# Inverse square roots of the query and key scales by Newton steps on VectorE, no row form of the first norm, and four PSUM banks for the first two projections

## The chip, the cores and the metric

The kernel runs on one core of a Trainium2 chip. A core has five engines that work side by side, each through a queue of its own in order: TensorE (PE in the profile, with its weight loads apart as PEld), VectorE (DVE), ScalarE (ACT), GpSimd (POOL) and SyncE (SP, which only issues DMA transfers here). Matmul results lie in PSUM, which has eight banks; everything else lies in SBUF.

The metric is the device time of one execution in microseconds (us). The kernel before takes 1255.68 us, the median of three runs (1253.61 to 1256.59).

## The reference

A causal two-layer trunk over 512 tokens of width 1024, in float32. Layer 0 mixes tokens by attention, layer 1 by a gated short convolution; each is followed by a gated MLP of width 2816 with a width-3 causal convolution. What the change touches is the entrance of layer 0:

```python
def rms_norm(x, g):
    y = x * lax.rsqrt(jnp.mean(x * x, axis=-1, keepdims=True) + EPS)
    return y * g

xn = rms_norm(h, norm_g)                      # over 1024 features
proj = xn @ w_in                              # 1024 x (3*1024 + 8)
q, k, v = heads(...)                          # 16 heads of 64
q_fox = rms_norm(q[:, :8], fox_q_g)           # over 64 features, per head and token
k_fox = rms_norm(k[:, :8], fox_k_g)           # the same for the 8 stick-breaking heads
```

Heads 0 to 7 do softmax attention with a forget-gate decay added to the logits; heads 8 to 15 do stick-breaking attention, whose weights are a running product of sigmoids from the diagonal backwards. Every one of the later norms (before each MLP and before the convolution mixer) is the same `rms_norm`.

## The kernel before, in words

**Precision.** Each float32 matrix product is made of three fast matmuls: both factors are split into a high part (a rounded copy, by ACT) and a low part (the rest, by DVE), and high x high, high x low and low x high are added up in PSUM (`mm3`, `mm3_rhs`; L248, L473). A weight slice of 512 KB comes by DMA into a tile `raw` and is split into `whi` (L228) and `wlo` (L235). Each of these three has three buffers.

**Entrance.** x is loaded token by token and turned feature by feature by PE transposes (`take`, L672), each into a PSUM bank: tag `b` (four banks) for features 0 to 3, 6 and 7, tag `c` (two banks) for 4 and 5. Tag `a` has two banks. `keep` (L681) copies the bank to the residual stream `h` and so frees it. The norm's gain is multiplied into the split activations `hs_hi` and `hs_lo`; its scale per token, `norm.col`, is applied later, to the products. ACT sums the squares (`squares`, L688); `Norm.scale` (L280) makes the mean on DVE and calls `rsqrt`, which is one GpSimd instruction, a power of -0.5 (L313). For every norm, `spread` (L287) then turns the column of scales into a row by four PE transposes into a `c` bank (L291) and an ACT copy (`nrow`, L292). The rows of the later norms scale the projections of their layers (L774, L814 to L821). The scales of the first norm are used as a column only (L465, L481, L510), and by `rx2`, their squares over 64 (L480).

**Groups of heads.** Sixteen heads are four groups of four. Group g has three projections: `heads(0, g)` and `heads(1, g)` (keys and queries: 0 is keys) and `values(g)`, each over four blocks of 128 tokens and eight slices of features (`columns`, L446). Each block takes a PSUM bank of tag `a`. In `heads`, ACT copies the finished block out (L504) and squares it (L505), and DVE adds the squares per head (L507). At the end come two small DVE steps (L517, L518), the power on GpSimd (16 numbers on each partition, L519), and then, in `scale`, the product with `norm.col` (L510) and the scaling of both halves (L513). `turn_heads(p)` transposes a pair of heads (L530) and splits it (L534, L535). `logits`, `turn` and `weigh` are the attention steps of half a pair: logits in the `b` banks, softmax or the running product (L569 to L586), transposes of the weights in the `c` banks (L604), their split (L606, L609), and the product with the values (L628).

**What sets the order.** The source counts a clock of its own: every block of matmuls adds its estimated time (`spend`), `after(us, fn)` puts a step off until so much of that clock has gone by, and `flush` runs at once all that was put off. `scale` is put off by SCALE = 8.0. The attention steps u = 0 to 17 follow one another, and between them `fill(us)` draws as much work from a list of fillers: `values(0)`, then keys, queries and values of groups 1 to 3, then half of the output projection. `need(what)` draws fillers, half a microsecond at a time, until a step that it waits for has been written out. So:

```python
after(SCALE, scale)                   # L520, at the end of heads
need(("normed", i, p // 2))           # L526, at the head of turn_heads
```

The order of writing is not the order of an engine's queue. The framework plans each engine's queue with a cost model of its own: of the instructions that its model holds to be ready it takes the one written first, so that an instruction that isn't ready lets later ones pass. Once planned, the queue is fixed, and the chip waits wherever the model was too hopeful.

After the attention (`output(1)`, L764) come the MLP of layer 0, the convolution mixer and the MLP of layer 1.

Of the kernel before, what the change touches and what calls it, by code (L numbers as in the profile page):

```python
# [17 lines left out]
F32 = mybir.dt.float32  # L18
F32R = mybir.dt.float32r
BF16 = mybir.dt.bfloat16  # L20
I32 = mybir.dt.int32
# [4 lines left out]
P = 128  # L26
S = 512
NB = S // P
# [8 lines left out]
AHEAD = 2  # L37
PT = 2
PRE = 6.0
SCALE, SHARES, LATER = 8.0, 1.5, 1.5  # L40
SUM_STEP = 0.6
WARM = 34
HEADS = 4.0
# [5 lines left out]
def trunk(  # L49
# [71 lines left out]
    for i in range(2):  # L121
# [1 line left out]
        pool.memset(m, 0.0)  # L123
        pool.affine_select(out=m, in_=m, pattern=[[-1, P]], compare_op=ALU.is_ge, fill=MASKED, base=-i, channel_multiplier=1)
        masks.append(m)
    minus_half = const.tile([P, 16], F32, tag="minus_half", name="minus_half")
    pool.memset(minus_half, -0.5)
    ones = const.tile([P, 1], F32, tag="ones", name="ones")
    pool.memset(ones, 1.0)

# [50 lines left out]
    def after(us, fn):  # L181
        later.append((clock[0] + us, len(later), fn))
        later.sort(key=lambda e: e[0])
# [76 lines left out]
    class Norm:  # L260
# [19 lines left out]
        def scale(self, sums):  # L280
            v = tiny.tile([P, NB], F32, tag="nv", name=f"nv_{self.name}")
            dve.tensor_scalar(v, sums, 1.0 / D, EPS, op0=ALU.mult, op1=ALU.add)
            self.col = const.tile([P, NB], F32, tag="ncol", name=f"ncol_{self.name}", bufs=2)
            rsqrt(self.col, v)
            after(NROWS, self.spread)

        def spread(self):  # L287
            self.row = work.tile([P, S], F32, tag="nrow", name=f"nrow_{self.name}", bufs=1)
# [20 lines left out]
                    after(SUM_STEP, lambda: sums(b + 1, t))  # L309
            after(NSUMS, lambda: sums(0, bank("c")))  # L310

    def rsqrt(dst, v):
        pool.tensor_tensor(dst, v, minus_half[:, 0:v.shape[1]], op=ALU.pow)  # L313

    def split(hi, lo, src):
        act.activation(hi, src, AF.Copy)  # L316
# [126 lines left out]

    v_tiles = {}

    def columns(g, width=256):  # L446

        ws = [weights(), weights(AHEAD - 1)]
        for b in range(NB):
            acc = bank("a")  # L450
            tok = slice(b * P, (b + 1) * P)
            for k in range(ND):
                w = ws[k // 4]
                mm3_rhs(acc[:, 0:width], (hs_hi[:, k, tok], hs_lo[:, k, tok]), (w[0][:, k % 4, :], w[1][:, k % 4, :]), k == 0, k == ND - 1)
                spend(0.36)
                yield b, acc, k == ND - 1
# [37 lines left out]
    def heads(i, g):  # L494

        kept = [work.tile([P, 2, 256], F32, tag=("u0", "u1")[i], name=f"qk{i}{g}{j}", bufs=2 + i) for j in range(2)]
        total, r = (tiny.tile([P, NB, 4], F32, tag=n, name=f"{n}{i}{g}") for n in ("qv", "qr"))
        for b, acc, last in columns(g):
            yield 1
            if not last:  # L500
                continue
            if b % 2 == 0:
                sq = work.tile([P, S], F32, tag="sq", name=f"sq_{i}{g}{b}").rearrange("p (b h d) -> p b h d", b=2, d=HD)
            act.activation(kept[b // 2][:, b % 2, :], acc[:, 0:256], AF.Copy)  # L504
            act.activation(sq[:, b % 2], acc[:, 0:256].rearrange("p (h d) -> p h d", d=HD), AF.Square)  # L505
            if b % 2:
                dve.tensor_reduce(total[:, b - 1:b + 1, :], sq, axis=AX.X, op=ALU.add)  # L507

        def scale():
            dve.tensor_tensor(r, r, norm.col[:, :, None].to_broadcast([P, NB, 4]), op=ALU.mult)  # L510
            for j, t in enumerate(kept):
                t = t.rearrange("p b (h d) -> p b h d", d=HD)
                dve.tensor_tensor(t, t, r[:, 2 * j:2 * j + 2, :, None].to_broadcast([P, 2, 4, HD]), op=ALU.mult)  # L513
            normed[i, g] = kept
            done.add(("normed", i, g))

        dve.tensor_tensor(total, total, rx2[:, :, None].to_broadcast([P, NB, 4]), op=ALU.mult)  # L517
        dve.tensor_scalar(total, total, EPS, None, op0=ALU.add)  # L518
        rsqrt(r.rearrange("p b h -> p (b h)"), total.rearrange("p b h -> p (b h)"))  # L519
        after(SCALE, scale)  # L520

    def turn_heads(p):
# [377 lines left out]
```

## Time and profile before

| | |
|---|---|
| median of three runs | 1255.68 us |
| the profiled execution | 1255.41 us, of which the span from first to last instruction is 1253.7 us |
| PE busy | 1212.9 us (97% of the span) |
| DVE busy | 747.1 us (60%) |
| ACT busy | 500.5 us (40%) |
| POOL busy | 49.6 us (4%) |
| mean granted TensorE clock | 0.986 |
| the power (L313) with 16 numbers a partition, x8 | median 2900 ns, 24.8 us together |
| the power with 4 numbers a partition, x4 | median 1007 ns, 4.1 us together |

A row of the timeline gives the start in us from the first instruction, the duration, the engine, the line, the operation with its tiles, and how often it was repeated; in square brackets stands how long the engine had been idle, and whose end released it. A row of the windows gives for a stretch of the span its length, then for PE, PEld, DVE, ACT and POOL the busy time with the number of instructions, then the TensorE clock that was granted (1.00 is full speed), the share of the DMA engines and GB/s.

### The profile page before, as it was taken

What the parts mean: (1) busy time and instruction counts of PE and PEld (TensorE: products, weight loads), DVE (VectorE), ACT (ScalarE), POOL (GpSimd) and SP (SyncE); (2) the same over time, 40 slices, a digit from 0 to 9 for tenths busy, and PEclk for the clock granted to TensorE, in tenths of its full rate; (3) what the DMA queues carried; (4) which work ended last, traced back from release to release, by engine and by line L of the source; (5) the groups of instructions that cost most, each with busy time, mean ns of one, the idle gap of its engine ahead of it and who ended that gap; (6) DMA issues with size and microseconds to landing.
All of it is one profiled execution on the core that took longest, in us unless ns stands there. A gap on an engine that the chain in (4) does not pass through costs nothing.

```text
span 1253.7 us, 15395 instructions
## 1 busy us (share of the span) xinstructions
PE 1212.9 (97%) x6133; PEld 1008.8 (80%) x6133; DVE 747.1 (60%) x1104; ACT 500.5 (40%) x815; POOL 49.6 (4%) x114
## 2 busy tenths in 40 slices
PE   7989999987999999999999999999999999999998
PEld 7978988766888888888888888888888888888886
DVE  4575677886676777765333455555667777772312
ACT  5454566554444344443222222233343444432120
POOL 3211111100000000000000000000000000000000
PEclk8998999997999999999999999999999999999999
DMA  5321221210323333333333323323233333332330
GB/s 157 93 61 34 69 62 40 68 51 18 100 85 101 95 91 101 88 93 93 93 93 97 101 85 100 99 87 100 85 101 96 89 101 89 96 101 84 104 115 34
DMA packets 175272, 108.15 MB, mean 86 GB/s; under 512 B 4604, under 2 KB 168492, under 8 KB 175200
## 3 DMA queue, kind: packets, MB, share of 16 engines
q1 hardware_dynamic: 174944, 107.01, 28.7%
q8 instruction: 48, 0.79, 0.3%
q0 software_dynamic: 256, 0.16, 0.1%
q14 instruction: 24, 0.20, 0.0%
HBM read 105.06 MB, written 2.10 MB: 85 GB/s over the span
## 4 chain that ended last, share of the span: by engine, by line
PE 87%; DVE 7%; ACT 3%; POOL 1%; DMA 1%; issue 1%; SPq 0%; DVEq 0%; ACTq 0%
PE psb L250 11%; PE psb L252 11%; PE psa L250 11%; PE psb L251 11%; PE psa L252 11%; PE psa L251 11%; PE psa L474 4%; PE psa L476 4%; PE psa L475 4%; PE psb L474 2%; PE psb L475 2%; PE psb L476 2%; DVE rest L585 2%; POOL qr L313 1%; PE psc L604 1%; PE psb L552 1%
## 5 line engine op out<-in xcount | busy, mean ns | idle before, releaser
L228 ACT ACTIVATE whi<-raw 128x1024 fp32r<-128x1024 f32 (+2 forms) x198 | 208.4, 1053 | 357.8 <-PE psb L251 131.1
L235 DVE TENSOR_TENSOR wlo<-raw,whi 128x1024 fp32r<-128x1024 f32 (+2 forms) x198 | 240.3, 1214 | 178.1 <-ACT whi L228 177.3
L250 PE MATMUL psb<-hs_hi,whi 128*128 128x512 f32 x480 | 189.9, 396 | 0.0
L252 PE MATMUL psb<-hs_hi,wlo 128*128 128x512 f32 x480 | 189.8, 395 | 0.0
L251 PE MATMUL psb<-hs_lo,whi 128*128 128x512 f32 x480 | 188.7, 393 | 0.0
L250 PE MATMUL psa<-hs_hi,whi 128*128 128x512 f32 x416 | 164.7, 396 | 0.0
L252 PE MATMUL psa<-hs_hi,wlo 128*128 128x512 f32 x416 | 164.2, 395 | 0.0
L251 PE MATMUL psa<-hs_lo,whi 128*128 128x512 f32 x416 | 163.9, 394 | 0.0
L324 DVE SCALAR_TENSOR_TENSOR u<-y,taps,u 128x510 f32<-128x510 f32 (+1 forms) x176 | 131.0, 747 | 3.0
L474 PE MATMUL psa<-whi,hs_hi 128*128 128x256 f32 (+1 forms) x384 | 114.0, 298 | 3.8 <-ACT sq L505 1.9
L476 PE MATMUL psa<-whi,hs_lo 128*128 128x256 f32 (+1 forms) x384 | 110.9, 289 | 0.0
L475 PE MATMUL psa<-wlo,hs_hi 128*128 128x256 f32 (+1 forms) x384 | 110.6, 288 | 0.0
L251 PEld LDWEIGHTS psb<-hs_lo,whi 128*128 128x128 f32 x480 | 90.1, 188 | 21.4
L252 PEld LDWEIGHTS psb<-hs_hi,wlo 128*128 128x128 f32 x480 | 90.1, 188 | 21.4
L250 PEld LDWEIGHTS psb<-hs_hi,whi 128*128 128x128 f32 x480 | 90.3, 188 | 20.3
L252 PEld LDWEIGHTS psa<-hs_hi,wlo 128*128 128x128 f32 x416 | 78.1, 188 | 18.6
L251 PEld LDWEIGHTS psa<-hs_lo,whi 128*128 128x128 f32 x416 | 78.1, 188 | 18.4
L250 PEld LDWEIGHTS psa<-hs_hi,whi 128*128 128x128 f32 x416 | 78.2, 188 | 18.0
L774 DVE TENSOR_TENSOR y<-psb,nrow_n 128x512 f32<-128x512 f32 x44 | 30.4, 691 | 83.9 <-PE psb L252 83.9
L474 PEld LDWEIGHTS psa<-whi,hs_hi 128*128 128x128 f32 x384 | 75.0, 196 | 5.0 <-ACT sq L505 2.2
L316 ACT ACTIVATE a<-u 128x512 fp32r<-128x512 f32 x44 | 27.8, 631 | 118.7 <-DVE u L779 118.7
L475 PEld LDWEIGHTS psa<-wlo,hs_hi 128*128 128x128 f32 x384 | 75.0, 195 | 0.0
(202 smaller groups left out, 1918.2 us busy)
## 6 DMA issues: line engine op xcount, KB each, us to landing
raw<-in_ffn_w_up SPq DMA_DIRECT2D x88, 512.0 KB, 3.8
raw<-in_ffn_w_down SPq DMA_DIRECT2D x30, 512.0 KB, 3.5
raw<-in_attn_w_in SPq DMA_DIRECT2D x24, 512.0 KB, 4.3
raw<-in_conv_w_in SPq DMA_DIRECT2D x24, 512.0 KB, 3.8
raw<-in_ffn_w_down SPq DMA_DIRECT2D x16, 448.0 KB, 3.6
raw<-in_attn_w_out SPq DMA_DIRECT2D x8, 512.0 KB, 3.4
raw<-in_conv_w_out SPq DMA_DIRECT2D x8, 512.0 KB, 4.0
x_tok<-in_x SPq DMA_DIRECT2D x4, 512.0 KB, 7.9
```

The lines of the kernel that those rows point to most:

```text
L228: made = act.activation(hi[:, 0:nk * n], raw[:, 0:nk * n], AF.Copy)
L235: dve.tensor_tensor(lo[:, 0:nk * n], raw[:, 0:nk * n], f32(hi[:, 0:nk * n]), op=ALU.subtract)
L250: pe.matmul(acc, w[0], rhs[0], start=first, stop=False)
L251: pe.matmul(acc, w[0], rhs[1], start=False, stop=False)
L252: pe.matmul(acc, w[1], rhs[0], start=False, stop=last)
L316: act.activation(hi, src, AF.Copy)
L324: dve.scalar_tensor_tensor(dst[:, d:], src[:, 0:S - d], tap(j), dst[:, d:], op0=ALU.mult, op1=ALU.add)
L474: pe.matmul(acc, lhs[0], w[0], start=first, stop=False)
L475: pe.matmul(acc, lhs[0], w[1], start=False, stop=False)
L476: pe.matmul(acc, lhs[1], w[0], start=False, stop=last)
L585: dve.tensor_tensor_scan(back, back, back, 1.0, op0=ALU.mult, op1=ALU.bypass)
L774: dve.tensor_tensor(y, acc, norm.row, op=ALU.mult)
```

## The change

`rsqrt` no longer calls GpSimd. It writes twelve DVE instructions: half of the value, the integer shift and subtraction that give a first guess, and three Newton steps of three instructions each. The constant tile `minus_half` goes. The first norm (`n0`) no longer calls `spread`. In `columns`, the bank tag of each token block is now a parameter, and `heads(0, 0)` and `heads(1, 0)` take `a`, `a`, `b`, `b` in place of `a` four times. In `heads`, the two small DVE steps and `rsqrt` move into `scale`, which is put off by SCALE = 1.2 instead of 8.0, and the product with `norm.col` and the scaling of both halves move into a second step, `scaled`, put off by another 1.2 from there.

```diff
-SCALE, SHARES, LATER = 8.0, 1.5, 1.5
+SCALE, SHARES, LATER = 1.2, 1.5, 1.5
...
-    minus_half = const.tile([P, 16], F32, tag="minus_half", name="minus_half")
-    pool.memset(minus_half, -0.5)
...
-            rsqrt(self.col, v)
-            after(NROWS, self.spread)
+            rsqrt(self.col, v, NB, self.name)
+            if self.name != "n0":
+                after(NROWS, self.spread)
...
-    def rsqrt(dst, v):
-        pool.tensor_tensor(dst, v, minus_half[:, 0:v.shape[1]], op=ALU.pow)
+    def rsqrt(dst, v, n, name):
+
+        def t(tag, dt=F32):
+            return tiny.tile([P, n], dt, tag=f"{tag}{n}", name=f"{tag}_{name}", bufs=2)
+        half = t("rh")
+        dve.tensor_scalar(half, v, -0.5, None, op0=ALU.mult)
+        shifted = t("rs", I32)
+        dve.tensor_scalar(shifted, v.bitcast(I32), 1, None, op0=ALU.logical_shift_right)
+        guess = t("rg", I32)
+        dve.tensor_scalar(guess, shifted, -1, 0x5F3759DF, op0=ALU.mult, op1=ALU.add)
+        y = guess.bitcast(F32)
+        for i in range(3):
+            a = t("ra")
+            dve.tensor_tensor(a, y, y, op=ALU.mult)
+            b = t("rb")
+            dve.tensor_tensor(b, a, half, op=ALU.mult)
+            z = dst if i == 2 else t("ry")
+            dve.scalar_tensor_tensor(z, b, 1.5, y, op0=ALU.add, op1=ALU.mult)
+            y = z
...
-    def columns(g, width=256):
+    def columns(g, width=256, tags="aaaa"):
...
-            acc = bank("a")
+            acc = bank(tags[b])
...
-        for b, acc, last in columns(g):
+        for b, acc, last in columns(g, tags="aaaa" if g else "aabb"):
...
         def scale():
+            dve.tensor_tensor(total, total, rx2[:, :, None].to_broadcast([P, NB, 4]), op=ALU.mult)
+            dve.tensor_scalar(total, total, EPS, None, op0=ALU.add)
+            rsqrt(r.rearrange("p b h -> p (b h)"), total.rearrange("p b h -> p (b h)"), 16, f"qk{i}{g}")
+            after(SCALE, scaled)
+
+        def scaled():
             dve.tensor_tensor(r, r, norm.col[:, :, None].to_broadcast([P, NB, 4]), op=ALU.mult)
...
-        dve.tensor_tensor(total, total, rx2[:, :, None].to_broadcast([P, NB, 4]), op=ALU.mult)
-        dve.tensor_scalar(total, total, EPS, None, op0=ALU.add)
-        rsqrt(r.rearrange("p b h -> p (b h)"), total.rearrange("p b h -> p (b h)"))
         after(SCALE, scale)
```

## The prediction, made before the changed kernel was run

> **What bounds the kernel now.** First the page's shares by engine, then a table of windows that cuts the span into its stages.
>
> ```profile
> span 1253.7 us, 15395 instructions
> PE 1212.9 (97%) x6133; PEld 1008.8 (80%) x6133; DVE 747.1 (60%) x1104; ACT 500.5 (40%) x815; POOL 49.6 (4%) x114
> 21.30:24.80 3.50, 0.61 (x5) 0.60 (x4) 0.75 (x4) 2.61 (x7) 1.04 (x1) 0.71 0.46 133
> 24.80:45.00 20.20, 20.20 (x155) 20.01 (x154) 6.75 (x11) 7.73 (x17) 3.38 (x2) 0.88 0.20 54
> 45.00:130.00 85.00, 75.67 (x605) 71.25 (x604) 56.30 (x141) 42.54 (x103) 11.81 (x15) 0.94 0.24 67
> 130.00:200.00 70.00, 68.03 (x571) 63.14 (x570) 49.53 (x116) 42.29 (x109) 10.01 (x22) 1.00 0.17 49
> 200.00:250.00 50.00, 44.55 (x350) 40.33 (x350) 41.72 (x77) 30.25 (x74) 8.65 (x18) 1.00 0.20 64
> 250.00:306.00 56.00, 44.57 (x252) 35.48 (x250) 42.38 (x76) 29.04 (x67) 2.95 (x17) 0.88 0.13 39
> 331.00:1253.00 922.00, 918.54 (x3987) 743.00 (x3985) 517.79 (x637) 317.95 (x399) 3.02 (x3) 1.00 0.31 93
> ```
>
> From 331 us on PE is busy 918.5 of 922 us at full clock: there a change can only cost. All that can be won lies before: 2.9 us of idle PE at 21.3, and 9.3, 2.0, 5.4 and 11.4 us in the four attention stages, with granted clocks of 0.71, 0.88, 0.94 and 0.88 beside them. In 200 to 250 DVE is busy 83% of the time, almost as much as PE.
>
> **The power on GpSimd.** The line's own view says how long it takes and who waits.
>
> ```profile
> L313 POOL TENSOR_TENSOR qr<-qv,minus_half x8: 2899/2900/3804, 36.1 to 225.3; 128x16 f32<-128x16 f32 x8
> L313 POOL TENSOR_TENSOR ncol_n<-nv_n,minus_half x4: 1006/1007/1045, 23.1 to 884.5; 128x4 f32<-128x4 f32 x4
>   DVE qr L510: 18.9, 8
> ```
>
> Eight times out of eight DVE stands still for it, 18.9 us together: the planner puts L510 close behind, because its model holds the power to be short, and DVE's queue can't pass it.
>
> **Part A, the first norm and the four banks.** PE, ACT and DVE rows around the gap, then two windows:
>
> ```profile
> 21.04 0.28 PE L476 MATMUL psa<-whi,hs_lo 128*128 128x256 f32 x1
> 24.20 0.90 PE L291 MATMUL psc<-ident,ncol_n 128*128 128x128 f32 x3 [2.89 <-POOL ncol_n L313]
> 24.76 0.56 PE L474 MATMUL psa<-whi,hs_hi 128*128 128x256 f32 x1
> 29.60 0.30 PE L474 MATMUL psa<-whi,hs_hi 128*128 128x256 f32 x1
> 17.44 0.68 DVE L686 COPY h<-psb 128x512 f32<-128x512 f32 x1
> 18.16 0.58 ACT L684 ACTIVATE h<-psb 128x512 f32<-128x512 f32 x1
> 22.97 0.39 ACT L505 ACTIVATE sq<-psa 128x256 f32<-128x256 f32 x1
> 24.00:29.60 5.60, 5.39 (x25) 5.40 (x26) 0.92 (x3) 0.60 (x1) 0.15 (x1) 0.50 0.00 0
> 30.00:35.00 5.00, 5.00 (x45) 5.00 (x44) 2.28 (x4) 3.35 (x6) 0.00 (x0) 1.00 0.00 1
> ```
>
> PE has finished two token blocks at 21.1 and then waits for the column of scales, only to transpose it into a row that nothing reads. Without `spread` alone, PE would still wait until 22.97 + 0.39 = 23.36, when ACT, which is squaring x until then, has emptied the first `a` bank. With banks `a a b b` the third block needs a `b` bank, and features 2 and 3 left theirs at 18.12 and 18.74. So the next matmul starts behind 21.04 at about 21.16 in place of 24.76: 3.6 us. Then the clock: in 24.0 to 29.6 it is 0.50. From 24.76 to 29.60 PE issues some 21 matmuls (25 in the window, four of them transposes) in 4.84 us; at the 0.111 us of the next window (5.00 us, 45) they take 2.4. Another 2.4 us. Sum A = 6.0 us. Lower end 24.76 - 23.5 = 1.3 us, should a bank not be free; the upper end is the sum itself, there being no more idle time or slow clock in these rows. It passes on in full, since PE is dense to 45. The twelve DVE steps of this norm take 2.4 us where the power took 1.0, and so end some 1.4 us after 24.2; their first reader is L517 behind `heads(0, 0)`, whose four blocks then end near 27.
>
> The Trainium skill ("TensorE: Matmul & The Clock Gate", Part 1: The HAM clock gate) lets the clock fall after an idle window of some 3.4 us. By that rule a gap of 2.89 us would not have halved the clock and A would be 3.6 us. The window of 0.50 right behind the gap says otherwise here.
>
> **Part B, eight chains on DVE.** DVE rows: two steps that depend on each other, two that don't, and one chain around the power.
>
> ```profile
> 24.18 0.16 DVE L481 TENSOR_TENSOR rx<-ncol_n 128x4 f32<-128x4 f32 x1 [1.16 <-POOL ncol_n L313]
> 24.38 0.17 DVE L482 TENSOR_SCALAR rx<-rx 128x4 f32<-128x4 f32 x1
> 45.88 0.17 DVE L517 TENSOR_TENSOR qv<-qv,rx 128x16 f32<-128x16 f32 x1
> 45.98 0.42 DVE L144 COPY taps<-psc 128x264 f32<-128x264 f32 x1
> 84.88 0.17 DVE L518 TENSOR_SCALAR qv<-qv 128x16 f32<-128x16 f32 x1
> 88.06 0.18 DVE L510 TENSOR_TENSOR qr<-qr,ncol_n 128x16 f32<-128x16 f32 x1 [3.01 <-POOL qr L313]
> ```
>
> A small step that needs the one before starts 0.20 us after it; with another instruction in between, it takes up 0.10 us of the queue. The before shows no integer step; I take it at the same price. From L518 to L510 it is 3.18 us now. Twelve steps alone make 0.2 + 12 x 0.20 = 2.6 us (0.6 saved); interleaved they occupy 12 x 0.10 + 0.1 = 1.3 us (1.9 saved). Over eight chains that is 4.6 to 15 us of DVE's queue, but only what reaches PE counts. PE's gaps behind three of the stalls:
>
> ```profile
> 89.77 0.44 PE L552 MATMUL psb<-qk_hi,qk_hi 64*128 64x384 f32 x1 [1.49 <-ACT w L571]
> 92.11 0.58 PE L474 MATMUL psa<-whi,hs_hi 128*128 128x256 f32 x1 [1.91 <-ACT sq L505]
> 112.20 0.66 PE L530 MATMUL psc<-ident,qk 128*128 128x128 f32 x4 [2.01 <-DVE qk_lo L535]
> 113.90 0.38 PE L474 MATMUL psa<-whi,hs_hi 128*128 128x256 f32 x1 [1.05 <-DVE v L468]
> 233.55 0.66 PE L530 MATMUL psc<-ident,qk 128*128 128x128 f32 x4 [1.80 <-DVE qk_lo L535]
> 237.37 0.38 PE L628 MATMUL psa<-pt,v 128*128 128x256 f32 x1 [1.32 <-DVE v L468]
> 87.00:97.00 10.00, 6.60 (x36) 6.11 (x35) 6.60 (x21) 4.42 (x15) 1.61 (x5) 0.70 0.11 39
> ```
>
> They sum to 9.6 us, and the clock of 0.70 in 87 to 97 costs another (97 - 92.11) x 0.5 = 2.4. Three chains shortened by 0.6 to 1.9 us give 1.7 to 5.7 us, up to 12 with all gaps and the cold stretch. I take 4, near the interleaved end, since 45.88 to 45.98 shows the planner slipping a copy between L517 and its dependent. The other five chains give nothing: PE has fillers then. POOL loses its powers, and what is queued behind them there, the memsets of L614, comes earlier; nobody waits for those now.
>
> The Trainium skill ("VectorE: DVE Perf Modes", Rules for kernel authors) speaks against the change: every DVE instruction pays a pipeline flush, so their number should be small. By it interleaving would win nothing, and B would stay at its lower price, 1.7 us. The row at 45.98, which starts 0.07 us before the one at 45.88 ends, doesn't bear that out for independent steps.
>
> **Part C, the order of writing.** SCALE = 8.0 forces fillers: counted with the source's 0.36 us a step, `heads(1, 1)` ends at 67.4 of the source's clock, `turn_heads(2)` is reached at 71.4 and `need` draws 4.3 us of `values(1)` until `scale` is due at 75.7. With 1.2 twice, `scaled` is written at 71.0, and nothing is forced. (For group 0 the forced 7.6 us become 2.5, but all of `values(0)` is drawn before the decay anyway; groups 2 and 3 force 1.1 us either way.) Counted to the end, fillers run out at 226.0 in place of 222.3, with the loop ending at 230.6 in both: 3.7 us of filler move into the bare tail. There PE has this:
>
> ```profile
> 293.48 1.11 PE L604 MATMUL psc<-ident,w 128*128 128x128 f32 x4 [6.71 <-DVE pt L609]
> 286.00:306.00 20.00, 12.45 (x58) 10.10 (x56) 12.40 (x24) 8.66 (x21) 1.17 (x6) 0.66 0.09 26
> ```
>
> A gap of 6.71 us with a clock of 0.66 in the twenty around it. If the 3.7 us fill it, C = 3.7 us; if a gap of 3.0 spares the clock, up to 0.34 x 12.45 = 4.2 more; if the planner draws them earlier, nothing. I take 2.
>
> **Part D, the later norms.** The three rows still come from a column, now twelve DVE steps where one power was.
>
> ```profile
> 884.24 0.15 DVE L282 TENSOR_SCALAR nv_n<-psc 128x4 f32<-128x4 f32 x1
> 887.56 0.60 PE L291 MATMUL psc<-ident,ncol_n 128*128 128x128 f32 x4
> ```
>
> The steps end at 884.4 + 12 x 0.20 = 886.8 and the transposes start at 887.56. Nothing, hidden behind PE's matmuls of the next layer. If a weight split of 1.2 us slips in between, PE waits 0.5 us, three times 1.5. The removed memset, ACT's copy for `n0` and the POOL time are off every path.
>
> **The sum.** 6.0 + 4 + 2 = 12.0 us. The profiled execution took 1255.41 us (1.7 around its span), 0.3 below the median, so 1243.4 us, and about 1243.5 beside the median runs.
>
> **The rivals.** First, only A arrives (the DVE steps take what the stalls took, and the planner's new order eats C): 1255.4 - 6.0 = 1249.4 us. For it: 96 steps at 0.20 are 19.2 us against 18.9 of stalls. Against: the planner does interleave. Second, more arrives: A, all of B with its cold stretch (12) and C with the clock (up to 4 of its 7.9) make 22, so 1233. It needs that no new gap opens. Third, slower, by one mechanism: the planner puts some other DVE instruction between any two Newton steps, so a chain takes 12 x (0.10 + 0.54) = 7.7 us in place of 3.0 (0.54 = 41.72 / 77 in 200 to 250). Then the queries of four groups come 4.7 us late, and PE waits in `turn_heads`: 18.8 us lost, 6.0 won, 1268 us. It decides once the chain is longer than the room until the logits read these tiles: by the source's clock 83.5 - 71.9 = 11.6 us, and since the planner knows these steps' length, it would put other matmuls first. I hold it for unlikely but for group 0, where little other work is left. Fourth, the banks don't come free in the planner's eyes: A falls to 1.3, with half of B and C 1251 us. Last, a reshuffled queue gives all of it back, 1255.
>
> **How the numbers follow.** The forecast (1238 to 1249, its own range) 0.50; only A 0.22; more 0.10; the banks 0.02; all given back 0.05; slower 0.11. About 0.2% (2.5 us) is what a measurement of this kernel can tell from no change. Faster 0.50 + 0.22 + 0.10 + 0.02 = 0.84, same 0.05, slower 0.11. The range 1234 to 1253 leaves out the slower rival, the one without gain and the far half of "more", 0.20 in all.
>
> **What would show it.** A: no PE gap of over 1 us between 12.5 and 40, a granted clock of 1.00 from 16 on, the matmuls of the third block near 21.2. B: no wait of DVE for POOL; twelve steps between L518 and L510 in 1.5 to 4 us; the sum of PE's gaps in 45 to 290 down by 3 to 6 us. DVE's busy time up by 144 x 0.17 = 24 us to about 771, POOL's down by 29 to about 21. C: the gap before the last transposes under 4 us. D: no gap of PE after the output projection. The forecast is wrong if PE waits for L513 or L535 longer than before, or if PE's gaps between 45 and 306 keep their 28 us.

## The result, and the profile after

The changed kernel takes 1243.50 us (median of four runs, 1243.21 to 1248.89), beside 1255.78 us for the kernel before on the same chip. The ratio of their means is 0.9915, 95% interval 0.9886 to 0.9945, so 10.7 us less (6.9 to 14.3). The medians lie 12.3 us apart, because one of the four executions took 1248.89 us at a mean clock of 0.985 where the others had 0.992 to 0.993. The prediction was 1243.5 us.

First the page's shares by engine and the table of windows, for the stretches that were read before. The columns are the same as ahead of the prediction.

```profile
span 1241.7 us, 15526 instructions
PE 1207.4 (97%) x6129; PEld 1002.8 (81%) x6129; DVE 765.5 (62%) x1248; ACT 500.3 (40%) x814; POOL 21.2 (2%) x101
```

```profile
24.80:45.00 20.20, 20.20 (x173) 20.01 (x172) 15.14 (x50) 8.64 (x17) 0.00 (x0) 1.00 0.44 131
45.00:130.00 85.00, 79.13 (x661) 72.33 (x659) 65.49 (x185) 48.99 (x126) 3.64 (x18) 1.00 0.18 51
130.00:200.00 70.00, 66.30 (x550) 62.69 (x551) 55.35 (x146) 42.42 (x106) 3.48 (x19) 0.98 0.22 61
200.00:250.00 50.00, 42.84 (x318) 38.20 (x317) 38.25 (x81) 28.31 (x64) 2.00 (x12) 0.97 0.14 43
250.00:306.00 56.00, 48.31 (x252) 38.59 (x251) 43.27 (x75) 29.84 (x64) 2.57 (x14) 0.94 0.16 47
331.00:1241.00 910.00, 906.55 (x3928) 732.62 (x3926) 515.99 (x653) 314.10 (x394) 0.00 (x0) 1.00 0.31 93
```

From 24.8 to 45 PE is busy without a pause at full clock (0.88 before). The long last stage idles for 910.00 - 906.55 = 3.45 us, as before (922.00 - 918.54 = 3.46). Between lie the four attention stages. From 45 to 130 PE's idle time fell from 9.3 to 5.9 us, and the clock rose from 0.94 to 1.00. From 130 to 200 idle time rose from 2.0 to 3.7 and the clock fell from 1.00 to 0.98; from 200 to 250 idle time rose from 5.4 to 7.2 and the clock fell from 1.00 to 0.97. From 250 on idle time fell from 11.4 to 7.7. So something was gained early and part of it was lost again later.

Two instructions that both kernels have mark how far each is. These are PE rows of the kernel before, the transposes for the forget-gate decay and the first matmul of the output projection after the attention:

```profile
65.25 0.63 PE L431 MATMUL psc<-ident,fwide 128*128 128x128 f32 x4 [0.83 <-DVE fwide L425]
306.34 0.48 PE L250 MATMUL psa<-o_hi,whi 128*128 128x512 f32 x1 [0.49 <-DVE o L639]
```

And PE rows of the changed kernel: the start of the third token block, which now goes into a `b` bank, the same two marks, and between them the long gaps of the attention.

```profile
21.23 0.28 PE L490 MATMUL psb<-whi,hs_hi 128*128 128x256 f32 x1
...
58.80 0.63 PE L447 MATMUL psc<-ident,fwide 128*128 128x128 f32 x4 [0.91 <-DVE fwide L441]
...
159.50 0.38 PE L490 MATMUL psa<-whi,hs_hi 128*128 128x256 f32 x1 [2.47 <-DVE v L484]
...
222.10 0.41 PE L490 MATMUL psa<-whi,hs_hi 128*128 128x256 f32 x1 [4.93 <-DVE v L484]
...
256.33 0.65 PE L248 MATMUL psa<-o_hi,whi 128*128 128x512 f32 x1 [2.04 <-DVE o L658]
...
282.09 0.66 PE L623 MATMUL psc<-ident,w 128*128 128x128 f32 x4 [2.64 <-DVE pt L628]
...
294.23 0.47 PE L248 MATMUL psa<-o_hi,whi 128*128 128x512 f32 x1 [0.56 <-DVE o L658]
```

At the decay the changed kernel is 65.25 - 58.80 = 6.45 us ahead, at the end of the attention 12.11, at the end of the span 12.0. So in these two traces 6.45 us come from the entrance, 5.66 from the attention, and nothing from what follows. The gap before the last transposes went from 6.71 to 2.64 us. But gaps of 2.47 and 4.93 us, each in front of a projection of values, are new: PE waits there until DVE has emptied a bank (L484).

### The profile page after: what moved, and what is told of

It is laid out like the page before. It is cut to its first block, busy times and chain, and to the rows that moved or that the text cites. A ratio compares the mean times of both kernels' runs of the same rounds, so it can differ in the third digit from the quotient of the medians.

```text
span 1241.7 us, 15526 instructions
## 1 busy us (share of the span) xinstructions
PE 1207.4 (97%) x6129; PEld 1002.8 (81%) x6129; DVE 765.5 (62%) x1248; ACT 500.3 (40%) x814; POOL 21.2 (2%) x101
## 4 chain that ended last, share of the span: by engine, by line
PE 88%; DVE 7%; ACT 3%; issue 1%; DMA 1%; SPq 0%; DVEq 0%; ACTq 0%
PE psb L248 11%; PE psb L250 11%; PE psb L249 11%; PE psa L248 11%; PE psa L249 11%; PE psa L250 11%; PE psa L490 4%; PE psa L492 4%; PE psa L491 4%; PE psb L492 2%; PE psb L491 2%; PE psb L490 2%; DVE rest L604 1%; PE psc L623 1%; ACT whi L226 1%; DVE wlo L233 1%
## 5 line engine op out<-in xcount | busy, mean ns | idle before, releaser
L250 PE MATMUL psa<-hs_hi,wlo 128*128 128x512 f32 x416 | 164.3, 395 | 0.0
L490 PE MATMUL psa<-whi,hs_hi 128*128 128x256 f32 (+1 forms) x352 | 102.7, 293 | 10.7 <-DVE v L484 7.7
L491 PE MATMUL psa<-wlo,hs_hi 128*128 128x256 f32 (+1 forms) x352 | 100.6, 286 | 0.4 <-DVE wlo L233 0.4
L492 PE MATMUL psa<-whi,hs_lo 128*128 128x256 f32 (+1 forms) x352 | 100.9, 287 | 0.0
L490 PEld LDWEIGHTS psa<-whi,hs_hi 128*128 128x128 f32 x352 | 67.4, 192 | 13.1 <-DVE v L484 8.6
L491 PEld LDWEIGHTS psa<-wlo,hs_hi 128*128 128x128 f32 x352 | 67.6, 192 | 0.6 <-DVE wlo L233 0.6
```

What stands on the lines that cost most here:

```text
L250: pe.matmul(acc, w[1], rhs[0], start=False, stop=last)
L490: pe.matmul(acc, lhs[0], w[0], start=first, stop=False)
L491: pe.matmul(acc, lhs[0], w[1], start=False, stop=False)
L492: pe.matmul(acc, lhs[1], w[0], start=False, stop=last)
```

## The experiments

Each experiment was timed in five rounds beside the kernel before on the same chip. A difference in us from the kernel before is worked out from the ratio and that run's time of before; two changed versions are compared by their medians. "The old order" is SCALE = 8.0 with the two small steps and `rsqrt` at the end of `heads`.

The traces are compared by three marks that all of them have: the 4x4 transpose of `heads_in` near 20 us, the transposes for the decay near 60, and the first matmul of the output projection after the attention near 300. From the first to the second mark is called the entrance here, from the second to the third the attention. A window from mark to mark holds the same work of PE (1619 or 1620 matmul records in the attention). Its length less PE's busy time is idle time; where PE is busy longer for the same matmuls, it ran at a lower clock. A trace is one execution, and its start differs from one to another, so stages are read from traces and totals from the ratios.

### Part A by its halves: no row (a_spread), four banks (a_banks), both (a_both)

```diff
-            after(NROWS, self.spread)
+            if self.name != "n0":
+                after(NROWS, self.spread)
```

```diff
-            acc = bank("a")
+            acc = bank(tags[b])
...
-        for b, acc, last in columns(g):
+        for b, acc, last in columns(g, tags="aaaa" if g else "aabb"):
```

> The kernel before with one edit: the first norm no longer calls spread. Additive theory (the steps of the prediction add up): PE no longer waits for the column, but still for the first bank of tag a, which ACT empties at 23.36; the third block starts near 23.5 in place of 24.76, a gap of some 2.2 us stays in front of it and the clock still falls. About 1.3 us faster (1254). Rival (a gap has to last longer for the clock to fall): the stretch of half clock goes too and it is 3.7 us faster (1252).

> The kernel before with one edit: heads(0, 0) and heads(1, 0) take banks a a b b; the first norm still makes its row. Additive theory: the four transposes stay in PE's queue, but if the planner puts them behind matmuls that are ready, PE loses no time to them and the gain is part A without 0.5 us of transposes, 5.5 us (1250). Rival (the banks help only together with the missing row): the transposes stay where they were, PE waits for the column as before, and the time is 1255 to 1256.

> The kernel before with both edits of part A: no row of the first norm, and banks a a b b. The power stays on GpSimd and the order of writing is the old one. Additive theory: 6.0 us faster, 1249.7, with PE dense from 12.5 to 45 and no half clock after 16 until the old gap at 90. Rival (only the reshuffled queue counts): the end moves by another amount than the stretch to 45 does, by more than 2 us.

Measured: without the row 1254.85 us beside 1254.37, ratio 0.9997 (0.9988 to 1.0007), which is nothing. Four banks alone 1251.09, ratio 0.9979 (0.9970 to 0.9988), 2.6 us less (1.5 to 3.8). Both 1250.03, ratio 0.9965 (0.9953 to 0.9978), 4.4 us less (2.8 to 5.9).

PE rows of the kernel without the row of scales, each behind a gap, and a window behind the first:

```profile
23.98 0.38 PE L475 MATMUL psa<-whi,hs_hi 128*128 128x256 f32 x1 [1.51 <-ACT sq L506]
50.88 0.36 PE L475 MATMUL psa<-whi,hs_hi 128*128 128x264 f32 x1 [1.89 <-DVE gate L471]
```

```profile
25.00:28.50 3.50, 3.50 (x19) 3.50 (x18) 0.70 (x2) 0.00 (x0) 0.00 (x0) 0.51 0.31 83
```

PE now waits for ACT, which has to empty the `a` bank, as the prediction said of this half. The gap is 1.4 us shorter, and behind it stand 3.4 us at half clock where the kernel before has 6.8 (22.8 to 29.6). But a later gap has grown, from 0.81 us (before, at 51.98) to 1.89, and has a half-clock stretch of its own (52.4 to 55.8). The runs show no gain. With four banks alone the transposes of the row come behind more matmuls:

```profile
24.28 0.65 PE L291 MATMUL psc<-ident,ncol_n 128*128 128x128 f32 x4 [0.76 <-POOL ncol_n L313]
```

The gap shrinks to 0.76 us. The expected gain was 5.5 us; the entrance of this trace is 4.59 us shorter, and the runs give 2.6. With both edits there is no gap. The windows of the entrance say how much (before, then both):

```profile
20.31:65.25 44.94, 40.41 (x314) 39.53 (x314) 20.33 (x48) 21.05 (x41) 8.52 (x6) 0.92 0.34 95
```

```profile
21.79:60.74 38.95, 37.31 (x310) 36.63 (x310) 20.32 (x48) 20.45 (x40) 8.52 (x6) 1.00 0.39 109
```

The entrance takes 44.94 us in the kernel before and 38.95 with both: 5.99 us less, the sum of part A. The runs show 4.4, with 5.9 as the upper end. In this trace 1.48 us are lost ahead of the first mark, which stands at 21.79 in place of 20.31: the half-clock stretch at the start is 6.8 us long (10.3 to 17.1), and 3.4 in the kernel before (12.5 to 15.9). Whether that is what takes the rest in the runs isn't shown.

### Part B alone (b_newton)

```diff
-    def rsqrt(dst, v):
-        pool.tensor_tensor(dst, v, minus_half[:, 0:v.shape[1]], op=ALU.pow)
+    def rsqrt(dst, v, n, name):
...
+        dve.tensor_scalar(half, v, -0.5, None, op0=ALU.mult)
...
```

The twelve DVE steps stand where the power stood, in the old order, with the row and two banks.

> The kernel before with Newton steps on DVE for all twelve inverse roots, written at the old place (the small steps at the end of heads, scale put off by 8.0); the first norm keeps its row and the first groups keep banks a. Additive theory (part B): no stall of DVE for GpSimd, the attention's PE gaps down by 1.7 to 5.7 us; but PE's first wait for the column grows by the 1.4 us that twelve steps take longer than the short power. 2 to 3 us faster, 1252 to 1254. Rival (the steps take what the stalls took): no gain, 1255.5 to 1257. Rival (all of the gaps behind the stalls go, with the cold stretch): 10 us faster, 1246.

Measured: 1245.51 us, ratio 0.9931 (0.9918 to 0.9944), 8.7 us less (7.0 to 10.3). More than the 2 to 3 expected, and near the rival of 10. Its first gap, and its windows around the first of the three pairs of gaps that the prediction summed, then over the entrance and the attention:

```profile
24.91 0.39 PE L491 MATMUL psa<-whi,hs_hi 128*128 128x256 f32 x1 [2.09 <-ACT sq L522]
```

```profile
87.00:97.00 10.00, 10.00 (x86) 9.42 (x87) 8.36 (x16) 5.91 (x12) 0.00 (x0) 1.00 0.10 23
21.81:62.91 41.10, 38.04 (x314) 37.13 (x314) 25.80 (x84) 21.05 (x41) 0.00 (x0) 1.00 0.37 103
62.91:295.92 233.01, 210.67 (x1619) 187.79 (x1620) 187.16 (x448) 134.73 (x335) 11.40 (x62) 0.98 0.18 51
```

The attention of the kernel before:

```profile
65.25:306.34 241.09, 214.21 (x1619) 192.09 (x1620) 177.82 (x376) 134.51 (x335) 29.32 (x68) 0.95 0.17 49
```

From 87 to 97 PE was busy for 6.60 us at a clock of 0.70 before; it is now busy throughout at 1.00. Around the second pair, from 112 to 120, the clock was 0.79 and is 1.00. The whole attention is 8.08 us shorter, 4.54 of them idle time (26.88 to 22.34) and 3.54 PE being busy for less long with the same matmuls. Of the 9.6 us in the prediction's six gaps 5.1 are left: the first and the third are gone, the second is 0.68 and the fourth 1.48 us, and the third pair stays, with 1.67 and 1.31. So B takes some gaps away, and the slow clock behind the first two pairs with them. The entrance, too, is 3.84 us shorter, which the expectation didn't have: the gap there is 2.09 us in place of 2.89, and the clock doesn't fall. The two stages make 11.9 us; this trace starts 1.5 us later than the one of before, and the runs give 8.7.

### Part C alone (c_order)

```diff
-SCALE, SHARES, LATER = 8.0, 1.5, 1.5
+SCALE, SHARES, LATER = 1.2, 1.5, 1.5
...
         def scale():
+            dve.tensor_tensor(total, total, rx2[:, :, None].to_broadcast([P, NB, 4]), op=ALU.mult)
...
+            rsqrt(r.rearrange("p b h -> p (b h)"), total.rearrange("p b h -> p (b h)"))
+            after(SCALE, scaled)
```

The new order of writing, with the power still on GpSimd.

> The kernel before with part C alone: the two small steps and the power (still on GpSimd) are written in scale, put off by 1.2, and the scaling in a second step, put off by another 1.2. The first norm keeps its row, all groups keep banks a. Prediction's part C: the tail gap of 6.71 us shrinks to some 3, 2 us faster (1252.5; between 0 and 8 us). Rival (the order alone wins nothing, since values written later are late on DVE and open new gaps that weigh the shorter tail up): 1253 to 1256.

Measured: 1272.62 us beside 1254.73, ratio 1.0146 (1.0128 to 1.0163), 18.3 us more. Rows of its waits (us in total, times, longest), DVE's between 20 and 310 us and PE's between 45 and 306, and its attention:

```profile
DVE qr L516 <- POOL qr L313: 24.1, 8, 3.0
PE psc L533 <- DVE qk L519: 13.4, 4, 4.2
66.25:320.58 254.33, 221.46 (x1619) 196.98 (x1620) 177.29 (x376) 135.34 (x335) 29.05 (x68) 0.95 0.17 47
```

DVE's standstills grow from 18.9 to 24.1 us, and they now reach `turn_heads`: PE waits 13.4 us for the scaled queries and keys, which it didn't before. That is the place that the prediction gave to its slower rival, with the power in the role of the stretched chain. Its price of 18.8 us meets the 18.3 in part by chance: it was four waits of 4.7 us, and the attention, 13.2 us longer, has 6.0 us more idle time, while PE is busy 7.3 us longer for the same matmuls. With the power the new order costs; its own worth has to be read with the Newton steps in place.

### A and B in the old order (ab), and the changed kernel beside it (after_again)

```diff
-SCALE, SHARES, LATER = 1.2, 1.5, 1.5
+SCALE, SHARES, LATER = 8.0, 1.5, 1.5
...
-            after(SCALE, scaled)
...
+        dve.tensor_tensor(total, total, rx2[:, :, None].to_broadcast([P, NB, 4]), op=ALU.mult)
+        dve.tensor_scalar(total, total, EPS, None, op0=ALU.add)
+        rsqrt(r.rearrange("p b h -> p (b h)"), total.rearrange("p b h -> p (b h)"), 16, f"qk{i}{g}")
         after(SCALE, scale)
```

(From the changed kernel; the tile `minus_half` is made again, but nothing reads it. The second is the changed kernel itself.)

> Parts A and B together, written in the old order (small steps at the end of heads, scale put off by 8.0): the changed kernel without C. If A (4.3 measured) and B (8.9 measured) add up in full, 13.2 us faster than before, 1241.2, and C as the changed kernel has it costs 1 to 2 us. If they share the half-clock stretch at 22.8 to 29.6, which the newton run alone also avoided (2.4 us and more), 10 to 11 us faster, 1243.5, and C is worth nothing. If C is worth the predicted 2 us, this kernel is 2 us slower than the changed one, 1245.5.

> The changed kernel once more, with more rounds, beside the others on the same chip: 10.7 us faster than before by the first comparison, between 7 and 14.

Measured: 1240.58 us without C, ratio 0.9886 (0.9872 to 0.9900); with C 1244.60, ratio 0.9925 (0.9907 to 0.9943). The intervals don't overlap: the changed kernel is 4.0 us slower than its own first two parts. A and B add up in the runs: 4.4 + 8.7 = 13.1, together 14.3 (12.5 to 16.1). In the traces they share a part of the entrance, which is 5.99 us shorter with A, 3.84 with B and 6.96 with both; the runs are too coarse to show it. Windows of A and B in the old order, entrance and attention, and its row ahead of the last transposes:

```profile
21.20:59.18 37.98, 37.07 (x310) 36.57 (x310) 25.83 (x84) 20.50 (x40) 0.00 (x0) 1.00 0.41 112
59.18:290.67 231.49, 209.12 (x1620) 186.60 (x1620) 187.12 (x448) 134.78 (x335) 11.41 (x62) 0.99 0.18 52
```

```profile
279.14 1.12 PE L622 MATMUL psc<-ident,w 128*128 128x128 f32 x4 [6.70 <-DVE pt L627]
```

The gap of the tail is still there, 6.70 us. So C did shorten it by 4.1 us, as predicted, and paid more elsewhere. The attention of the changed kernel, and two windows right behind its new gaps:

```profile
58.80:294.23 235.43, 212.14 (x1619) 190.13 (x1620) 184.77 (x448) 134.74 (x335) 11.69 (x62) 0.97 0.17 51
160.90:164.30 3.40, 3.40 (x18) 3.40 (x17) 1.94 (x4) 1.57 (x3) 0.00 (x0) 0.50 0.00 0
222.30:225.70 3.40, 3.40 (x17) 3.40 (x17) 2.09 (x5) 0.42 (x1) 0.00 (x0) 0.50 0.00 0
```

Each gap is followed by 3.4 us at half clock in which PE has dense work, 1.7 us apiece; a third such stretch lies behind the gap of 2.04 us, from 256.5 to 259.9. With the order alone exchanged the attention is 3.94 us longer. Only 0.9 us of that is idle time (23.29 against 22.37), so the shorter gap in the tail pays for nearly all of the new gaps; for 3.0 us PE is busy longer with the same matmuls. What C loses is mostly clock. The changed kernel's second trace says the same (235.27 us, PE busy 212.10). What moved shows in ACT's row of the first block of the values of group 2, where the first new gap lies, with A and B in the old order, and in the changed kernel:

```profile
150.32 0.48 ACT L485 ACTIVATE v<-psa,ncol_n 128x256 fp32r<-128x256 f32 x1 [1.35 <-PE psa L494]
```

```profile
157.12 0.47 ACT L483 ACTIVATE v<-psa,ncol_n 128x256 fp32r<-128x256 f32 x1
```

With the new order these values come 6.8 us later, in among the attention steps that were written ahead of them. The fillers that are no longer forced were values of group 1; that the lag is carried on from there to groups 2 and 3, where the new gaps are, fits the rows but wasn't traced step by step.

### Chains of twice as many Newton steps (long)

```diff
-        for i in range(3):
+        for i in range(6):
...
-            z = dst if i == 2 else t("ry")
+            z = dst if i == 5 else t("ry")
```

The changed kernel with three more Newton steps, nine more DVE instructions, in each of twelve chains.

> The changed kernel with six Newton steps in place of three: nine more DVE instructions in every one of the twelve chains (the value is the same to rounding). Theory (steps slip in between other DVE work, at 0.10 to 0.20 us each, and PE has other work): the chains end 1 to 2 us later and the time grows by 0 to 3 us over the changed kernel. The prediction's slower rival (a chain's length is on PE's path through turn_heads): 8 chains times 1.8 us, 10 to 15 us slower than the changed kernel.

Measured: 1247.75 us, ratio 0.9947 (0.9932 to 0.9962), 3.2 us over the changed kernel, just above the 0 to 3 expected. A row of PE:

```profile
101.37 0.58 PE L490 MATMUL psa<-whi,hs_hi 128*128 128x256 f32 x1 [3.86 <-DVE v L484]
```

It doesn't cost the 10 to 15 us of a chain on PE's path, so the slower rival falls for the chain as it is. What comes of the 9 x 12 = 108 instructions is one more gap of the kind in question: values wait for a bank.

### How far the order is at fault (sc4, sc24, ab_f16)

The changed kernel with SCALE = 4.0; A and B in the old order with SCALE = 2.4 in place of 8.0; A and B in the old order with fewer fillers drawn in the last attention steps, so that more are left for the tail:

```diff
-SCALE, SHARES, LATER = 1.2, 1.5, 1.5
+SCALE, SHARES, LATER = 4.0, 1.5, 1.5
```

```diff
-SCALE, SHARES, LATER = 8.0, 1.5, 1.5
+SCALE, SHARES, LATER = 2.4, 1.5, 1.5
```

```diff
-FILL1, FILL2, FILL3 = 1.0, 4.4, 2.6
+FILL1, FILL2, FILL3 = 1.0, 4.4, 1.6
```

(The first diff is against the changed kernel, the other two are against A and B in the old order.)

> The changed kernel with SCALE = 4.0 in place of 1.2: the Newton steps are still written in scale, but the two put-offs make 8.0 together, so need forces group 1's fillers as before (source clock: turn_heads(2) at 76.9, fillers end at 222.3). Theory 1 (part C costs through the order of the fillers: values are written later against the attention steps and their PSUM banks are emptied late): the time falls to that of parts A and B alone, 1240 to 1242. Theory 2 (C costs because the small steps themselves are written later): it stays at 1244 to 1246.

> Parts A and B with SCALE = 2.4 in place of 8.0: the small steps at the end of heads, as before, and the scaling put off by 2.4, so that fillers are forced as little as in the changed kernel (turn_heads(2) at 71.9, fillers end at 225.8). Theory 1 (order of the fillers): 1243 to 1246, with gaps of 2 to 5 us in front of blocks of values. Theory 2 (lateness of the small steps): 1239 to 1241.

> Parts A and B with one constant changed, FILL3 = 1.6 in place of 2.6: all is written as before up to step u = 12, and from there the last half output projection is drawn more slowly, so that fillers end at 225.8 of the source's clock in place of 222.3. This is the tail of part C without its values. If the prediction's tail is right, the gap of 6.7 us shrinks to about 3 and this is 3 to 7 us faster than parts A and B, 1234 to 1238. If DVE, not the missing filler, sets the tail's length, 1240 to 1242.

Measured, beside 1253.64 for before: SCALE = 4.0 1242.22, ratio 0.9906 (0.9891 to 0.9921); SCALE = 2.4 in the old order 1249.88, 0.9969 (0.9956 to 0.9981); fewer fillers 1239.68, 0.9887 (0.9873 to 0.9900). A row of PE from the first, a row and the attention from the second, then the tail of the third, PE and DVE:

```profile
282.47 1.12 PE L623 MATMUL psc<-ident,w 128*128 128x128 f32 x4 [6.70 <-DVE pt L628]
```

```profile
162.33 0.49 PE L492 MATMUL psa<-whi,hs_hi 128*128 128x256 f32 x1 [2.38 <-DVE v L486]
59.62:302.35 242.73, 218.61 (x1620) 194.87 (x1620) 184.99 (x448) 134.91 (x335) 11.51 (x62) 0.94 0.17 49
```

```profile
278.43 1.12 PE L622 MATMUL psc<-ident,w 128*128 128x128 f32 x4 [6.12 <-DVE pt L627]
273.76 1.20 DVE L235 TENSOR_TENSOR wlo<-raw,whi 128x1024 fp32r<-128x1024 f32 x1
275.48 1.22 DVE L603 TENSOR_TENSOR_SCAN rest<-rest 128x511 f32<-128x511 f32 x1
```

With SCALE = 4.0 the long tail gap comes back and the time lies between the two orders; its interval overlaps both, so it tells them apart only by the trace. There PE waits 1.7 us, once, for a bank that DVE's L484 has to empty, in place of 7.7 us in the changed kernel, and the clock from 130 to 250 is 1.00. So the new gaps go when the fillers are forced again, although the small steps are written later still, as the first theory has it. When the old order forces fewer fillers, it loses 10 us (0.9969 beside 0.9886), more than the change did and more than either theory had, with a gap in front of the values at 162 although the small steps and the Newton steps stand early. So the loss doesn't need late small steps. Again it is mostly clock: the attention is 11.2 us longer than with SCALE = 8.0, of which 1.8 us is idle time and 9.5 PE being busy longer, with 27 us of the attention at half clock where the changed kernel has 14. Why slow stretches are so much more frequent there isn't settled. The third run speaks against C's idea itself: with 1.0 us of filler less in each step the tail gap is 6.12 in place of 6.70, and the time doesn't move. There DVE works without a pause from 269 on, most of it on scans and products of the last half pair, and by these rows it is that which sets when the last transposes can start.

### The bank of the values emptied by ScalarE (v_act)

```diff
-            act.activation(v[:, b, :, 0, :], src, AF.Copy, scale=r)
-            dve.scalar_tensor_tensor(v[:, b, :, 1, :], src, r, f32(v[:, b, :, 0, :]), op0=ALU.mult, op1=ALU.subtract)
...
+                vt = work.tile([P, S], F32, tag="sq", name=f"vt{g}{b}")[:, 0:256].rearrange("p (h d) -> p h d", d=HD)
+                act.activation(vt, src, AF.Copy, scale=r)
+                act.activation(v[:, b, :, 0, :], vt, AF.Copy)
+                dve.tensor_tensor(v[:, b, :, 1, :], vt, f32(v[:, b, :, 0, :]), op=ALU.subtract)
```

The changed kernel; only for groups 1 to 3. The bank is now read by ACT alone.

> The changed kernel, but for the values of groups 1 to 3 the bank is no longer read by VectorE: ScalarE copies the scaled block into a tile in SBUF, rounds the high part from there, and VectorE takes the low part from the two tiles. So a bank of the values is free after ScalarE's copy, and nothing on VectorE, Newton steps or scans, can hold it. Twelve copies more on ScalarE (about 0.4 us each, 5 us, of which little lies on PE's path). Theory (the new order costs about 4 us because the banks of the values are emptied late, by a VectorE instruction queued behind other work): the gaps of 2.47 and 4.93 us in front of the values at 159.5 and 222.1 us shrink under 1 us, the half-clock stretches behind them go, and the time falls by 3 to 6 us from the changed kernel's 1244.6, to 1239 to 1242. Rival (VectorE is simply behind there, and the bank is only where it shows): PE waits for the queries, the weights or the products a little later instead, and the time stays at 1243 to 1246. If ScalarE's extra copies reach PE's path, 1246 or more.

Why this is the suspect shows in rows of the changed kernel ahead of the gap at 222.10: ACT's copy of the finished block, and DVE's work up to the subtraction that empties the bank.

```profile
218.99 0.47 ACT L483 ACTIVATE v<-psa,ncol_n 128x256 fp32r<-128x256 f32 x1
218.51 0.15 DVE L324 TENSOR_TENSOR ra_qk<-ry_qk 128x16 f32<-128x16 f32 x1
218.58 1.21 DVE L604 TENSOR_TENSOR_SCAN rest<-rest 128x511 f32<-128x511 f32 x1
...
221.57 0.47 DVE L484 SCALAR_TENSOR_TENSOR v<-psa,ncol_n,v 128x256 fp32r<-128x256 f32 x1
```

ACT is done with the block at 219.46, and for another 2.1 us the subtraction stands behind a scan, products and Newton steps.

Measured: 1238.17 us beside 1254.32, ratio 0.9870 (0.9849 to 0.9891). That is 6.4 us below the changed kernel's 1244.60 (0.9925, 0.9907 to 0.9943), and as fast as A and B in the old order or faster; those two intervals overlap. PE's waits between 45 and 306 us, changed kernel and this one, and the attention of this one:

```profile
PE psa L490 <- DVE v L484: 7.7, 3, 4.9
```

```profile
PE psa L496 <- ACT vt L488: 2.2, 2, 1.6
PE psc L555 <- DVE qk L541: 3.8, 4, 1.7
```

```profile
59.36:291.60 232.24, 214.00 (x1619) 190.72 (x1620) 185.14 (x448) 140.39 (x347) 11.78 (x62) 0.96 0.18 51
```

The wait for a bank falls from 7.7 to 2.2 us; the two gaps are 0.62 and 1.55 us now, of which only the first is under the expected 1 us, and the half-clock stretches behind them are gone. Some of it comes back as a wait for the queries (1.7 to 3.8 us), as the rival had it, but not all: PE's idle time in the attention falls by 5.1 us, from 23.29 to 18.24. Half-clock stretches stand elsewhere in this trace (189.2, 250.7 and 278.0 us), so that it is only 3.2 us shorter; it is of an execution that took 1240.82 us, 2.7 above the median. So the late emptying of the bank is a cause of what the new order costs. That it is the only one isn't shown: PE idles 4.1 us less here than in the old order (22.37), so the edit gives more than C took, and the same edit in the old order, where PE waits 1.5 us for such a bank, wasn't run. This version has the lowest median of all that were run, with A and B in the old order, filled more slowly in the tail or not, next to it.

## Why the prediction was right, and where it was wrong

**The total** came out to the tenth, 1243.5, by luck. The sum was A 6.0 + B 4 + C 2 = 12.0. The runs give A 4.4, B 8.7, and C a loss of 4.0, which makes 9.1: wrong terms cancelled. The rest is the scatter of the measurement: the same kernel beside the other experiments had a median of 1244.60 us and a gain of 9.4.

**Part A** was right in mechanism, and by the trace in size; the runs give less. The third block starts at 21.23 (predicted near 21.2), no gap of over 1 us is left, the clock is 1.00, and the trace with A alone shows 5.99 us between two marks where the sum had 6.0. By the runs, 4.4 (2.8 to 5.9), it doesn't arrive in full, which the prediction took for granted. That the row alone gives nothing, because ACT holds the bank until 23.4, was in its lower end (1.3 us); the runs couldn't tell even that from zero (from 1.5 us faster to 0.9 slower), since the clock fell after the shorter gap too and another gap grew.

The Trainium skill ("TensorE: Matmul & The Clock Gate", Part 1: The HAM clock gate) has the clock judged by windows of about 3.4 us that run freely. The half-clock stretches here are 3.4 us long (160.90 to 164.30) or 6.8 (22.8 to 29.6, before), which agrees; a gap of 1.51 us was enough for one in one kernel, and gaps of 2.09 us in another and of 1.55 and 1.73 us within 5 us in a third weren't, which fits free-running windows. As a bound on what gap is harmless, an idle window of 3.4 us doesn't hold here.

**Part B** was right in the standstill and its removal, and too small by half: 4 us predicted, 8.7 measured. DVE has no wait for POOL left, and its busy time is 765.5 us (predicted about 771), POOL's 21.2; PE's idle time from 45 to 306 fell by 3.8 us (28.2 to 24.4, with C's loss in it). A chain of the changed kernel, DVE rows:

```profile
78.44 0.17 DVE L527 TENSOR_SCALAR qv<-qv 128x16 f32<-128x16 f32 x1
...
78.73 0.17 DVE L318 TENSOR_SCALAR rs_qk<-qv 128x16 int32<-128x16 int32 x1
78.93 0.17 DVE L320 TENSOR_SCALAR rg_qk<-rs_qk 128x16 int32<-128x16 int32 x1
...
79.65 0.28 DVE L588 TENSOR_REDUCE top<-psb 128x1 f32<-128x128 f32 x1
...
81.74 0.17 DVE L532 TENSOR_TENSOR qr<-qr,ncol_n 128x16 f32<-128x16 f32 x1
```

From L527 to L532 it is 3.3 us, no shorter than the 3.18 with the power, but useful work (L588) stands between the steps, as hoped. The step that failed is the pricing: "Three chains shortened by 0.6 to 1.9 us give 1.7 to 5.7 us". The 1.9 us is what a chain takes off DVE's queue, not what it becomes shorter by, and the chain shown here didn't become shorter. What was removed is a standstill of the whole queue. PE's idle time in the attention fell by 4.5 us, so the 4 was about right for the gaps, though for another reason. What the 4 left out is the clock: another 3.5 us in the attention, from the half-clock stretches behind the first two pairs of gaps. The first of these was in the bound of 12 "with all gaps and the cold stretch", the second nowhere. And 3.8 us of the trace lie at the entrance, which the prediction gave to A alone. In the attention the end of the standstills was worth 8.1 us, clock included, of 18.9 us of standstill in all.

The rule of the Trainium skill ("VectorE: DVE Perf Modes", Rules for kernel authors) that was weighed, by which every DVE instruction pays a flush and B keeps its lower price of 1.7 us, is not borne out: B gave 8.7. The 108 more instructions of the longer chains cost 3.2 us.

**Part C** was wrong in sign: +2 predicted, 4.0 lost. Its first half held: the gap before the last transposes went under 4 us (2.64). The step that failed is the end of its account, "3.7 us of filler move into the bare tail" at no cost to where they were. The forced fillers were values. Without them the attention steps are written ahead of the values, values come some 7 us later, DVE's queue has scans ahead of the subtraction that empties their banks, and PE waits 2.47 and 4.93 us, each time with 1.7 us of slow clock behind. The idle time nearly evens out against the tail (0.9 us more); the slow clock (3.0 us) is what is lost. With the emptying by ACT these two waits shrink, and the kernel takes 6.4 us less, which is more than C's loss. The prediction's own sign of error, that "PE waits for L513 or L535 longer than before", is a place to which the loss did not go: in the changed kernel PE waits for the first of them 1.7 us in all, 1.5 at most, and no longer for the second (4.8 us before).

**Part D** was right: the transposes of the later norms start without a gap, though twelve steps stand ahead. In one of them the last step on DVE starts at 874.22, and PE has no idle time ahead of the transposes:

```profile
875.30 0.60 PE L290 MATMUL psc<-ident,ncol_n 128*128 128x128 f32 x4
```

**The rivals.** "Only A" and "all given back" fall, since B alone gives 8.7. "More" was nearer to the truth for B, but its condition, that no new gap opens, failed. The slower rival's stretched chain did occur once, ahead of 222.10: it runs from 213.47 to 222.62, 9.2 us where the rival had 7.7, with scans of up to 1.2 us between its steps. What was held up there was the emptying of a bank more than `turn_heads`, with a gap of 4.93 us in place of 18.8 in all. (The chances outside the range add up to 0.21, not 0.20.)

**What stays open.** Why A and B in the old order with SCALE = 2.4 lose 10 us while the changed kernel with 1.2 twice loses 4: the traces put the difference down to the clock, but not to why it fell so often. How much of the 6.4 us of the emptying by ACT undoes C's loss, and how much the old order would have gained by it too. And what takes a part of A's 6.0 us in the runs.

## What to carry to other kernels

A standstill of an in-order queue was worth what PE did not get meanwhile, clock included, and not how much shorter the waiting chain became. When work is moved to fill a gap, look at who empties the banks of the work that is now late: a bank that only a busy engine can free is the next wait, and letting another engine free it can be worth more than the order. A gap in front of dense matmuls can cost more than its length, because of the slow clock behind it: C's new order cost 0.9 us of idle time and 3.0 of clock. So two versions with equal idle time need not be equally fast.

## What the runs showed of the hardware

The granted clock is halved in stretches of 3.4 us (160.9 to 164.3, changed kernel), or of a multiple: 6.8 us (22.8 to 29.6) and 13.7 us (289.0 to 302.7) in the kernel before. The length of a gap alone doesn't say whether one follows: behind a gap of 1.51 us one did in one kernel, and behind 2.09 us none did in another. An integer step of 16 numbers a partition on DVE (L318, L320 above) takes 0.17 us, as long as a float step, and the two, of which one needs the other, start 0.20 us apart.
